# A YOCO trunk on one core: MLPs, second pointwise and output product with the activations stationary, norms by tokens

## The chip, the core and the metric

The kernel runs on one core of one Trainium2 chip. The metric is the device time of one execution in microseconds (us). Every weight comes from HBM in fp32, once.

## What is computed

Two decoder layers on 256 tokens of 2048 features, everything in fp32. Each sub-layer ends with a norm over the features, `x = LN(ALPHA * x + f(x))`:

```python
def conv_module(x, ...):
    a, gate = jnp.split(x @ pw1_w + pw1_b, 2, axis=-1)
    h = a * jax.nn.sigmoid(gate)
    h = causal_depthwise_conv(h, dw_w, width=31) + dw_b
    h = jax.nn.silu(layer_norm(h, ln_g, ln_b))
    return h @ pw2_w + pw2_b

def sq_relu_mlp(x, w1, w2):          # 2048 -> 8192 -> 2048
    return jnp.square(jax.nn.relu(x @ w1)) @ w2
```

Layer 0 is the convolution module, then an MLP. Then K and V are computed once from the residual. Layer 1 is a dilated window attention of 16 heads (queries, three branches, output product `wo`), then an MLP.

## The kernel before

Every product is made in a split form: a weight or activation is the sum of an upper part (`hi`, rounded to the reduced fp32 type) and a lower part (`lo`, the rest), and three products hi*hi, hi*lo and lo*hi are added. Class `Weights` brings a weight in units of 128 x 1024 numbers: SP loads one into `raw`, ACT copies the upper part (`split_piece`, L117), and DVE, or POOL for units that `lo_engine` names, subtracts to get the lower part (L118). `get` keeps six units split ahead of the one in use.

The activations lie with features on partitions: `xres` is [128, 16 tiles, 256 tokens], and a product's input is [128, 16, 512], 256 columns of upper and 256 of lower parts. `fm_group` holds a 128 x 128 block of weights stationary and moves activations past it: for each input tile one matmul of 512 columns by the upper weight (L267) and one of 256 by the lower (L268). A block of 128 output features takes 16 input tiles; the last block of u1 and of the last residual uses three matmuls of 256 columns (`three`, L247 to L249). V alone is made with activations stationary: L690 to L692 move 512 columns of weights, three matmuls for an input tile and a half of the tokens.

An MLP goes through four quarters of its 8192 hidden features: 16 blocks of u1 (`w_1`), squared relu, 16 blocks of u2 (`w_2`) added into `xres` by DVE (L605, L607).

A norm needs sums across partitions. `ln_add` gathers sums on POOL while the last residual is made; then `ln_stats` sums across partitions on TensorE (L341, L343, L344), takes the power -1/2 on POOL (L351), spreads the result by TensorE (L353), and centres the tiles on DVE (L360) and POOL (L362); `ln_apply` scales, splits and writes the next input tile by tile on DVE and ACT (L368, L376, L381). `keep_warm` (L328) issues filler matmuls meanwhile. The last norm of the program is a list written by hand (L784 to L799) that ends with the stores.

The convolution before pw2 keeps DVE and POOL full; its norm ends in the SiLU, where each input tile of pw2 is made by DVE (L583, L584, L589).

## Time and profile before

| | us |
|---|---|
| three runs | 2221.66, 2222.25, 2223.79 (median 2222.25) |
| the profiled execution | 2221.38 |
| its span on the core | 2219.6 |
| TensorE / weight loads busy | 2166.1 / 1911.9 |
| DVE / ACT / POOL busy | 1459.1 / 1048.3 / 426.4 |

The span goes from the first to the last instruction of the core; the profiled execution's own time has 1.8 us around it. A busy TensorE is pipelined, so intervals between starts tell the pace better than the length of one matmul. In a row `xres<-mm,xres` reads "out<-in" by the names in the program; what stands in brackets is the idle time ahead of the instruction and what ended it.

### The profile page before, as it was taken

How to read it: one execution, taken by the hardware profiler on the slowest of the kernel's cores; microseconds unless marked ns; L12 is line 12 of the kernel's file. 1: busy time of each engine (PE TensorE's matmuls, PEld its weight loads, DVE VectorE, ACT ScalarE, POOL GpSimd, SP SyncE). 2: the span in 40 equal slices, each digit the busy share in tenths (PEclk: the TensorE clock that was granted, in tenths of full speed). 3: DMA queues.
4: the chain of work that ended last, by engine and by line, in shares of the span. 5: the costliest groups of instructions: out<-in, count | busy, mean ns of one | idle time of the engine just before them, and what ended most of it. 6: DMA issues, size and time to landing. Idle time of an engine off the chain costs nothing.

```text
span 2219.6 us, 33483 instructions
## 1 busy us (share of the span) xinstructions
PE 2166.1 (98%) x12915; PEld 1911.9 (86%) x12915; DVE 1459.1 (66%) x2206; ACT 1048.3 (47%) x1606; POOL 426.4 (19%) x338
## 2 busy tenths in 40 slices
PE   8899799999999999999999999999999999999997
PEld 7899688888888888888888888888888888888886
DVE  8999967655665665666744466677656656656664
ACT  6557445433443443444554455455434434434443
POOL 5598473000000000006300000640000000000054
PEclk9999999999999999999999999999999999999999
DMA  7364164656855555555465554536555555555552
GB/s 263 109 200 156 64 205 142 197 187 169 258 187 185 188 187 190 190 188 188 132 223 188 189 171 150 182 123 217 189 185 186 190 189 190 188 184 189 185 186 85
DMA packets 113264, 398.07 MB, mean 179 GB/s; under 512 B 12432, under 2 KB 16976, under 8 KB 113104
## 3 DMA queue, kind: packets, MB, share of 16 engines
q1 hardware_dynamic: 111040, 392.79, 54.1%
q10 hardware_dynamic: 2064, 3.15, 1.1%
q8 instruction: 101, 1.65, 0.3%
q14 instruction: 59, 0.48, 0.1%
HBM read 390.64 MB, written 5.24 MB: 178 GB/s over the span
## 4 chain that ended last, share of the span: by engine, by line
PE 86%; DVE 12%; DMA 1%; issue 1%; ACT 0%; SPq 0%; ACTq 0%; DVEq 0%
PE mm L267 51%; PE mm L268 26%; DVE s L467 4%; DVE act L467 2%; DVE o L467 2%; PE mm L692 1%; PE mm L690 1%; PE mm L691 1%; PE mm L249 1%; PE mm L248 1%; PE mm L247 1%; DVE s L471 1%; DVE act L584 0%; DVE xres L381 0%; DMA xres<-in_xt 0%
## 5 line engine op out<-in xcount | busy, mean ns | idle before, releaser
L267 PE MATMUL mm<-act,whi 128*128 128x512 f32 x4928 | 1734.2, 397 | 11.9 <-DVE act L584 6.1
L268 PE MATMUL mm<-act,wlo 128*128 128x256 f32 x4928 | 1380.7, 280 | 0.0
L118 DVE TENSOR_TENSOR wlo<-raw,whi 128x1024 fp32r<-128x1024 f32 (+1 forms) x676 | 835.9, 1239 | 592.4 <-ACT whi L117 570.4
L117 ACT CAST whi<-raw 128x1024 fp32r<-128x1024 f32 (+1 forms) x740 | 769.9, 1047 | 922.7 <-PE mm L267 553.4
L267 PEld LDWEIGHTS mm<-act,whi 128*128 128x128 f32 x4928 | 924.4, 188 | 235.8 <-DVE act L368 6.2
L268 PEld LDWEIGHTS mm<-act,wlo 128*128 128x128 f32 x4928 | 930.3, 189 | 0.8
L612 POOL TENSOR_TENSOR xres<-xres,npiv 128x256 f32<-128x256 f32 x8 | 7.0, 871 | 1585.2 <-ACT npiv L285 1585.2
L247 PE MATMUL mm<-act,whi 128*128 128x256 f32 x704 | 202.5, 288 | 5.9 <-ACT whi L117 5.6
L249 PE MATMUL mm<-act,wlo 128*128 128x256 f32 x704 | 201.2, 286 | 2.3 <-POOL wlo L118 2.1
L248 PE MATMUL mm<-act,whi 128*128 128x256 f32 x704 | 200.6, 285 | 0.1
L118 POOL TENSOR_TENSOR wlo<-raw,whi 128x1024 fp32r<-128x1024 f32 x64 | 155.6, 2464 | 39.9 <-ACT whi L117 39.9
L247 PEld LDWEIGHTS mm<-act,whi 128*128 128x128 f32 x704 | 136.4, 194 | 7.4 <-ACT whi L117 6.1
L249 PEld LDWEIGHTS mm<-act,wlo 128*128 128x128 f32 x704 | 136.2, 193 | 3.4 <-POOL wlo L118 2.5
L248 PEld LDWEIGHTS mm<-act,whi 128*128 128x128 f32 x704 | 136.4, 194 | 0.5 <-DVE act L234 0.3
L605 DVE TENSOR_TENSOR xres<-mm,xres 128x256 f32<-128x256 f32 x128 | 54.0, 423 | 88.1 <-PE mm L268 73.9
L300 POOL TENSOR_TENSOR ln_acc<-ln_acc,xres 128x256 f32<-128x256 f32 x56 | 82.9, 1480 | 95.7 <-DVE xres L607 95.7
L467 DVE SCALAR_TENSOR_TENSOR s<-act,dw,s 128x256 f32<-128x256 f32 x225 | 100.6, 480 | 0.1
L607 DVE TENSOR_TENSOR xres<-mm,xres 128x256 f32<-128x256 f32 x156 | 66.2, 424 | 5.1
L296 ACT ACTIVATE sq<-xres 128x256 f32<-128x256 f32 x60 | 25.2, 420 | 80.1 <-DVE xres L607 26.3
L467 DVE SCALAR_TENSOR_TENSOR act<-act,dw 128x256 f32<-128x256 f32 x56 | 57.5, 1034 | 0.1
L301 POOL TENSOR_TENSOR ln_acc<-ln_acc,sq 128x256 f32<-128x256 f32 x56 | 55.2, 985 | 0.0
L234 DVE TENSOR_TENSOR act<-v,act 128x256 fp32r<-128x256 f32 x120 | 50.2, 419 | 6.6 <-ACT act L233 6.6
(146 smaller groups left out, 1218.2 us busy)
## 6 DMA issues: line engine op xcount, KB each, us to landing
raw<-in_w SPq DMA_DIRECT2D x512, 512.0 KB, 4.2
raw<-in_w_pw SPq DMA_DIRECT2D x94, 512.0 KB, 4.3
raw<-in_w_v SPq DMA_DIRECT2D x32, 512.0 KB, 4.4
raw<-in_w_k SPq DMA_DIRECT2D x32, 512.0 KB, 3.6
raw<-in_w_q SPq DMA_DIRECT2D x32, 512.0 KB, 3.5
raw<-in_w_o SPq DMA_DIRECT2D x32, 512.0 KB, 4.4
scratch<-es ACTq DMA_DIRECT2D x1, 3072.0 KB, 35.2
bt<-scratch SPq DMA_DIRECT2D x16, 128.0 KB, 3.9
```

The source lines that it names most:

```text
L117: self.last_hi = self.nc.scalar.copy(out=hi[:, s], in_=r[:, s])
L118: self.lo_engine[i].tensor_tensor(out=lo[:, s], in0=r[:, s], in1=hi[:, s].bitcast(F32), op=ALU.subtract)
L247: nc.tensor.matmul(out=o, lhsT=hi, rhs=x[:, 0:T], start=kt == 0, stop=False)
L248: nc.tensor.matmul(out=o, lhsT=hi, rhs=x[:, T:2 * T], start=False, stop=False)
L249: nc.tensor.matmul(out=o, lhsT=lo, rhs=x[:, 0:T], start=False, stop=kt == KT - 1)
L267: nc.tensor.matmul(out=acc, lhsT=hi, rhs=x, start=kt == 0, stop=kt == KT - 1)
L268: W.last_mm = nc.tensor.matmul(out=acc[:, T:2 * T], lhsT=lo, rhs=x[:, 0:T], start=False, stop=kt == KT - 1, skip_group_check=True)
L300: nc.gpsimd.tensor_tensor(out=acc[:, 0:T], in0=acc[:, 0:T], in1=z, op=ALU.add)
L301: nc.gpsimd.tensor_tensor(out=acc[:, T:2 * T], in0=acc[:, T:2 * T], in1=sq, op=ALU.add)
L467: nc.vector.scalar_tensor_tensor(out=o, in0=tap, scalar=w, in1=o, op0=ALU.mult, op1=ALU.add)
L605: nc.vector.tensor_tensor(out=y, in0=acc[:, 0:T], in1=y, op=ALU.add)
L607: nc.vector.tensor_tensor(out=y, in0=acc[:, T:2 * T], in1=y, op=ALU.add)
```

## The change

pw2, both MLPs and the output product are now made like V, by `tm_chunk`: an input tile of 128 tokens is stationary and 512 columns of weights move, three matmuls (L299 to L301) for an input tile and a token half s. A chunk is 512 output features and uses eight weight units; four chunks make 2048 features. The residual `xres` is now [128 tokens, 2 halves, 2048 features]. The weights are laid out accordingly on the host, x is loaded a second time by tokens, and the output leaves by tokens.

Since the next product needs features on partitions, `turned` transposes 128 x 512 numbers by four transposes on TensorE (L314), ACT copies the upper part (L317) and DVE subtracts the lower (L318). `after(n, f)` and `tick` put such work n steps (of three matmuls) later. In the MLP the squared relu is ACT's relu and DVE's multiply (L695) on a chunk's half, turned six steps later.

A norm runs along the free axis: `bn_stats` as the chunks come (L617), `bn_aggr`, an addition on DVE (L620, L621) and a power on POOL (L622), then two operations on DVE for each chunk (`apply`, L627 and L629) with gain and bias from rows that SP loads to all partitions. In the last chunk ahead of a norm the last six input tiles are taken first for half 0, then for half 1 (`TAIL`); the first chunk behind it takes eight tiles of half 0 first (`HEAD`). `norm_between` sets after how many steps each apply and each turn comes. The filler matmuls of these norms are gone; those of the convolution's norm stay.

POOL gets the lower part of the first four units of pw2 (`POOL_2`) and of units 3 to 10 of the product behind each of three norms (`POOL_LN`), and the four additions of pw2's bias (L728). The last norm is `final`, by halves, with part of the work on ACT (L839) and POOL (L840, L841). pw1, the convolution, K, Q and the attention's products keep their form.

```diff
+TAIL = 10
+HEAD = 8
...
-TAIL_POOL = 2
+POOL_2 = 4
+POOL_LN = 8
...
+    def tm_units(dram_ap, c, js, lo_engine):
+        return [W.add(dram_ap[c, j, :, h * 1024:(h + 1) * 1024], lo_engine) for j in js for h in range(2)]
+    def mlp_units(layer):
+        return [([tm_units(w_1[layer], 4 * q + c, range(4), nc.vector) for c in range(4)],
+                 [tm_units(w_2[layer], c, range(4 * q, 4 * q + 4), nc.vector) for c in range(4)]) for q in range(NQ)]
+    def on_pool(units):
+        for u in units:
+            W.lo_engine[u] = nc.gpsimd
...
-    u_pw2 = fm_units(w_pw2, groups_of(KT, GRP), nc.vector)
+    u_pw2 = [tm_units(w_pw2, c, range(4), nc.vector) for c in range(4)]
+    on_pool(u_pw2[0][:POOL_2])
...
+    for u in (u_mlp[0][0][0][0], u_v[0], u_mlp[1][0][0][0]):
+        on_pool(range(u[0] + 3, u[0] + 3 + POOL_LN, 1))
...
+    both = [(kt, s) for kt in range(KT) for s in range(2)]
+    one_by_one = lambda a, b: [(kt, s) for s in range(2) for kt in range(a, b)]
+    tail_order = both[:2 * TAIL] + one_by_one(TAIL, KT)
+    head_order = one_by_one(0, HEAD) + both[2 * HEAD:]
+    def tm_chunk(units, x, evacuate, order=both):
+        accs = [bank(ps_mm, "mm") for _ in range(2)]
+        left = [4] * len(units)
+        seen = [0, 0]
+        for kt, s in order:
+            i, k = divmod(kt, 2)
+            hi, lo = W.get(units[i], units[min(j for j, n in enumerate(left) if n)])
+            hi, lo = hi[:, k * 512:(k + 1) * 512], lo[:, k * 512:(k + 1) * 512]
+            xh, xl = x[:, kt, s * P:(s + 1) * P], x[:, kt, T + s * P:T + (s + 1) * P]
+            nc.tensor.matmul(out=accs[s], lhsT=xh, rhs=hi, start=kt == 0, stop=False)
+            nc.tensor.matmul(out=accs[s], lhsT=xh, rhs=lo, start=False, stop=False)
+            nc.tensor.matmul(out=accs[s], lhsT=xl, rhs=hi, start=False, stop=kt == KT - 1)
+            left[i] -= 1
+            if not left[i]:
+                W.drop(units[i])
+            seen[s] += 1
+            if seen[s] == KT:
+                evacuate(s, accs[s])
+            tick()
+    def turned(src, dst, c, s):
+        ps = bank(ps_s, "s")
+        for j in range(4):
+            nc.tensor.transpose(out=ps[:, j * P:(j + 1) * P], in_=src[:, j * P:(j + 1) * P], identity=ident)
+        ps = ps.rearrange("p (j t) -> p j t", j=4)
+        hi, lo = (dst[:, 4 * c:4 * c + 4, o + s * P:o + (s + 1) * P] for o in (0, T))
+        nc.scalar.copy(out=hi, in_=ps)
+        nc.vector.tensor_tensor(out=lo, in0=ps, in1=hi.bitcast(F32), op=ALU.subtract)
...
+        def end(self, s):
+            nc.vector.bn_aggr(out=self.mv[s], in_=self.stats[s])
+            nc.vector.tensor_scalar(out=self.rs[s], in0=self.mv[s][:, 1:2], scalar1=EPS, scalar2=None, op0=ALU.add)
+            nc.gpsimd.tensor_tensor(out=self.rs[s], in0=self.rs[s], in1=npow[:, 0:1], op=ALU.pow)
...
+        def apply(self, s, c):
+            z = xres[:, s, chunk(c)]
+            t = tmp.tile([P, 512], F32, name="t", tag="b")
+            nc.vector.scalar_tensor_tensor(out=t, in0=z, scalar=self.mv[s][:, 0:1], in1=self.g[:, chunk(c)],
+                                           op0=ALU.subtract, op1=ALU.mult)
+            nc.vector.scalar_tensor_tensor(out=z, in0=t, scalar=self.rs[s], in1=self.b[:, chunk(c)],
+                                           op0=ALU.mult, op1=ALU.add)
...
+    def norm_between(norm, dst):
+        def turn_later(n, s, c):
+            after(n, lambda: turned(xres[:, s, chunk(c)], dst, c, s))
+        def at_end(s):
+            norm.end(s)
+            if s == 0:
+                norm.apply(0, 0)
+                after(4, lambda: norm.apply(0, 1))
+                turn_later(5, 0, 0)
+                turn_later(8, 0, 1)
+            else:
+                after(2, lambda: norm.apply(1, 0))
+                after(4, lambda: norm.apply(1, 1))
+                turn_later(5, 1, 0)
+                turn_later(7, 1, 1)
+                for n, c, half in ((8, 2, 0), (10, 2, 1), (12, 3, 0), (15, 3, 1)):
+                    after(n, lambda c=c, half=half: norm.apply(half, c))
+                    turn_later(n + 2, half, c)
+        return at_end
...
-            def evacuate(b, acc, h_hl=h_hl):
...
-            for u in u1:
-                fm_group(u, lambda kt: x_hl[:, kt, :], evacuate, single=u[0][0] == KT - 1)
-            residual(u2, lambda kt, h_hl=h_hl: h_hl[:, kt, :], q == 0, q == NQ - 1, ln)
+                def evacuate(s, acc, c=c, h_hl=h_hl):
+                    r = tmp.tile([P, 512], F32, name="r", tag="a")
+                    v = tmp.tile([P, 512], F32, name="v", tag="b")
+                    nc.scalar.activation(out=r, in_=acc, func=AF.Relu)
+                    nc.vector.tensor_tensor(out=v, in0=acc, in1=r, op=ALU.mult)
+                    after(6, lambda: turned(v, h_hl, c, s))
+                if q == 0 and c == 0:
+                    with tc.manual_schedule(engines={ACT, DVE, POOL}):
+                        tm_chunk(u1[c], x_hl, evacuate, head_order)
+                else:
+                    tm_chunk(u1[c], x_hl, evacuate)
...
+                nc.gpsimd.tensor_tensor(out=y, in0=y, in1=gb[:, 0, c * 1024:(c + 1) * 1024], op=ALU.add)
...
+    def final(norm):
+        def at_end(s):
+            norm.end(s)
+            for c in (0, 1):
+                norm.apply(s, c)
+                nc.sync.dma_start(out=out[s, :, chunk(c)], in_=xres[:, s, chunk(c)])
+            nb = small.tile([P, 1], F32, name="nb")
+            nc.vector.tensor_scalar(out=nb, in0=norm.mv[s][:, 0:1], scalar1=norm.rs[s], scalar2=-1.0,
+                                    op0=ALU.mult, op1=ALU.mult)
+            for c in (2, 3):
+                z = xres[:, s, chunk(c)]
+                if s == 1 and c == 2:
+                    norm.apply(s, c)
+                else:
+                    nc.scalar.activation(out=z, in_=z, func=AF.Identity, scale=norm.rs[s], bias=nb)
+                    nc.gpsimd.tensor_tensor(out=z, in0=z, in1=norm.g[:, chunk(c)], op=ALU.mult)
+                    nc.gpsimd.tensor_tensor(out=z, in0=z, in1=norm.b[:, chunk(c)], op=ALU.add)
+                nc.sync.dma_start(out=out[s, :, chunk(c)], in_=z)
+        return at_end
```

How the change moves instructions, at three places.

TensorE at the norm between pw2 and the first MLP. Before, from the end of pw2 (L247 to L249) to the first MLP matmul (L267); `inv` is the constant of the mean, `s` and `o` are PSUM banks:

```order
L247 MATMUL mm<-act,whi 128x256
L248 MATMUL mm<-act,whi 128x256
L249 MATMUL mm<-act,wlo 128x256
L328 MATMUL s<-whi 128x512 x2
L341 MATMUL mm<-inv,xres 128x1 x2
L343 MATMUL t<-inv,sq 128x1 x2
L344 MATMUL o<-xres,inv 128x256
L328 MATMUL s<-whi 128x512 x3
L353 MATMUL s<-ident,ln_rs 128x128 x2
L328 MATMUL s<-whi 128x512 x6
L267 MATMUL mm<-act,whi 128x512
L268 MATMUL mm<-act,wlo 128x256
```

Now, in the first chunk of the MLP: a step of three matmuls, the turn of a quarter of half 0, and three steps to the next turn:

```order
L314 MATMUL s<-ident,xres 128x128 x4
L299 MATMUL mm<-whi,act 128x512
L300 MATMUL mm<-wlo,act 128x512
L301 MATMUL mm<-whi,act 128x512
L299 MATMUL mm<-whi,act 128x512
L300 MATMUL mm<-wlo,act 128x512
L301 MATMUL mm<-whi,act 128x512
L299 MATMUL mm<-whi,act 128x512
L300 MATMUL mm<-wlo,act 128x512
L301 MATMUL mm<-whi,act 128x512
L314 MATMUL s<-ident,xres 128x128 x4
L299 MATMUL mm<-whi,act 128x512
```

The sums across partitions and the fillers are gone, and groups of four transposes stand among the matmuls of the next product.

POOL from the convolution's norm to the norm behind pw2. Before:

```order
L118 TENSOR_TENSOR wlo<-raw,whi 128x1024
L351 TENSOR_TENSOR ln_rs<-ln_var,npow 128x2
L362 TENSOR_TENSOR act<-act,ln_mc 128x256 x13
L118 TENSOR_TENSOR wlo<-raw,whi 128x1024 x2
L612 TENSOR_TENSOR xres<-xres,npiv 128x256
L619 TENSOR_TENSOR xres<-xres,npiv 128x256
L292 COPY ln_acc<-xres 128x256
```

Now:

```order
L380 TENSOR_TENSOR ln_rs<-ln_var,npow 128x2
L389 TENSOR_TENSOR act<-act,ln_mc 128x256 x13
L728 TENSOR_TENSOR xres<-xres,act 128x1024 x4
L622 TENSOR_TENSOR rs_3132<-rs_3132,npow 128x1
L119 TENSOR_TENSOR wlo<-raw,whi 128x1024 x3
L622 TENSOR_TENSOR rs_3133<-rs_3133,npow 128x1
L119 TENSOR_TENSOR wlo<-raw,whi 128x1024 x5
```

Two weight units of pw2 (L118) became four additions to `xres` (L728), and the eight weight units (L119) of the first MLP stand here, three of them between the powers (L622) of the two token halves.

DVE at the same norm, `t` and `act` being the scratch tile and the next input. Before:

```order
L605 TENSOR_TENSOR xres<-mm,xres 128x256
L349 TENSOR_SCALAR ln_var<-t,ln_m_3988 128x1 x2
L360 TENSOR_TENSOR xres<-xres,o 128x256 x3
L376 TENSOR_TENSOR t<-xres,s 128x256 x2
L381 TENSOR_SCALAR xres<-t,vec 128x256
L376 TENSOR_TENSOR t<-xres,s 128x256
L368 TENSOR_TENSOR act<-xres,act 128x256
L381 TENSOR_SCALAR xres<-t,vec 128x256
L368 TENSOR_TENSOR act<-xres,act 128x256
```

Now, from the statistics of half 1 on:

```order
L620 BN_AGGR mv_3131<-bn_3129 128x2
L621 TENSOR_SCALAR rs_3133<-mv_3131 128x1
L318 TENSOR_TENSOR act<-s,act 128x4x128
L627 SCALAR_TENSOR_TENSOR t<-xres,mv_3131,act 128x512
L629 SCALAR_TENSOR_TENSOR xres<-t,rs_3133,act 128x512
L627 SCALAR_TENSOR_TENSOR t<-xres,mv_3131,act 128x512
L629 SCALAR_TENSOR_TENSOR xres<-t,rs_3133,act 128x512
L318 TENSOR_TENSOR act<-s,act 128x4x128 x2
L627 SCALAR_TENSOR_TENSOR t<-xres,mv_3130,act 128x512
L629 SCALAR_TENSOR_TENSOR xres<-t,rs_3132,act 128x512
L318 TENSOR_TENSOR act<-s,act 128x4x128
L627 SCALAR_TENSOR_TENSOR t<-xres,mv_3131,act 128x512
```

Tile by tile work of 256 columns became pairs of 512 columns, each pair standing behind the lower part (L318) of a turn ahead of it.

## Rows read from the trace of the kernel before

**Rows 1.** The page, part 1: busy time, share of the span and instructions of each engine.

```profile
PE 2166.1 (98%) x12915; PEld 1911.9 (86%) x12915; DVE 1459.1 (66%) x2206; ACT 1048.3 (47%) x1606; POOL 426.4 (19%) x338
```

**Rows 2.** The page, part 4: the chain that ended last, share of the span by engine.

```profile
PE 86%; DVE 12%; DMA 1%; issue 1%; ACT 0%; SPq 0%; ACTq 0%; DVEq 0%
```

**Rows 3.** The page, part 5, weight units: xcount | busy us, mean ns | idle before.

```profile
L118 DVE TENSOR_TENSOR wlo<-raw,whi 128x1024 fp32r<-128x1024 f32 (+1 forms) x676 | 835.9, 1239 | 592.4 <-ACT whi L117 570.4
...
L117 ACT CAST whi<-raw 128x1024 fp32r<-128x1024 f32 (+1 forms) x740 | 769.9, 1047 | 922.7 <-PE mm L267 553.4
...
L118 POOL TENSOR_TENSOR wlo<-raw,whi 128x1024 fp32r<-128x1024 f32 x64 | 155.6, 2464 | 39.9 <-ACT whi L117 39.9
```

**Rows 4.** Timeline of TensorE at the marks: start us, us, engine, line, operation, xcount.

```profile
349.70 0.28 PE L249 MATMUL mm<-act,wlo 128*128 128x256 f32 x1
...
630.07 0.28 PE L249 MATMUL mm<-act,wlo 128*128 128x256 f32 x1
...
811.08 0.29 PE L249 MATMUL mm<-act,wlo 128*128 128x256 f32 x1
...
988.79 0.28 PE L249 MATMUL mm<-act,wlo 128*128 128x256 f32 x1
...
1080.14 0.28 PE L249 MATMUL mm<-act,wlo 128*128 128x256 f32 x1
...
1119.64 0.39 PE L692 MATMUL mm<-whi,act 128*128 128x512 f32 x1
...
1174.26 0.39 PE L267 MATMUL mm<-act,whi 128*128 128x512 f32 x1
...
1387.64 0.47 PE L267 MATMUL mm<-act,whi 128*128 128x512 f32 x1
...
1474.54 0.28 PE L249 MATMUL mm<-act,wlo 128*128 128x256 f32 x1
...
2203.63 0.28 PE L249 MATMUL mm<-act,wlo 128*128 128x256 f32 x1
```

**Rows 5.** Timeline of TensorE, 1304 to 1305 us, inside the attention.

```profile
1304.35 0.49 PE L744 MATMUL t<-ident,p 128*128 128x128 f32 x3
1304.67 0.39 PE L720 MATMUL s<-act,q 128*128 128x128 f32 x2
1304.90 0.60 PE L721 MATMUL s<-act,q 128*128 128x256 f32 x2
```

**Rows 6.** Timeline of DVE and of POOL, 263 to 274 us, the convolution's SiLU.

```profile
263.92 2.29 DVE L583 CAST act<-act 128x256 fp32r<-128x256 f32 x1
266.24 2.44 DVE L584 TENSOR_TENSOR act<-act 128x256 fp32r<-128x256 f32 x1
...
273.59 0.42 DVE L584 TENSOR_TENSOR act<-act 128x256 fp32r<-128x256 f32 x1
...
263.67 4.73 POOL L118 TENSOR_TENSOR wlo<-raw,whi 128x1024 fp32r<-128x1024 f32 x2 [5.25 <-ACT whi L117]
```

**Rows 7.** Groups by line and shape, columns as in rows 3.

```profile
L351 POOL TENSOR_TENSOR ln_rs<-ln_var,npow 128x2 f32<-128x2 f32 x5 | 3.5, 704 | 33.3 <-DVE ln_var L349 33.3
...
L784 DVE TENSOR_TENSOR xres<-xres,o 128x512 f32<-128x512 f32 x2 | 1.3, 683 | 0.6 <-ACT ln_mc L347 0.6
...
L696 ACT COPY act<-mm 128x512 f32<-128x512 f32 x8 | 4.6, 588 | 3.2 <-PE mm L692 2.9
```

**Rows 8.** Timeline of POOL at 155 us: an addition of 512 columns.

```profile
154.86 1.30 POOL L508 TENSOR_TENSOR ln_acc<-ln_acc,act 128x512 f32<-128x512 f32 x1
```

**Rows 9.** Timeline of DVE behind the last product; end of the chain that ended last.

```profile
2204.01 0.43 DVE L605 TENSOR_TENSOR xres<-mm,xres 128x256 f32<-128x256 f32 x1 [6.40 <-PE mm L249]
...
2213.98 0.64 ACTq L909
```

**Rows 10.** Windows: us, PE PEld DVE ACT POOL busy, PEclk, DMA share, GB/s.

```profile
55.00:66.00 11.00, 3.45 (x15) 3.27 (x16) 10.93 (x22) 0.80 (x2) 3.90 (x3) 0.53 0.39 128
...
356.00:362.00 6.00, 4.78 (x24) 3.71 (x25) 6.00 (x12) 3.80 (x7) 6.00 (x8) 1.00 0.00 0
```

More of the change, by code (lines that the diff above doesn't have):

```diff
@@ L273, in fm_group, with after, tick @@
                 W.drop(u)
+    later = []
+    def after(n, f):
+        later.append([n, f])
+    def tick():
+        for e in later:
+            e[0] -= 1
+        while True:
+            e = next((e for e in later if e[0] <= 0), None)
+            if e is None:
+                return
+            later.remove(e)
+            e[1]()
+    both = [(kt, s) for kt in range(KT) for s in range(2)]
[29 more added lines that the diff above has]
+        nc.vector.tensor_tensor(out=lo, in0=ps, in1=hi.bitcast(F32), op=ALU.subtract)
     def ln_begin():
@@ L622, in trunk, with load_rows @@
-    res_tile = lambda kt: xres[:, kt, :]
-    def norm(ln, g, b, unit):
-        rs = ln_stats(ln, res_tile, 3, unit)
-        x_hl = act.tile([P, KT, 512], F32R, name="act")
-        ln_apply(res_tile, rs, g, b, x_hl, unit)
-        return x_hl
+    chunk = lambda c: slice(c * 512, (c + 1) * 512)
+    def load_rows(*which):
+        r = act.tile([P, len(which), D], F32, name="act")
+        with tc.issue_after(W.last_load.ins):
+            for j, w in enumerate(which):
+                nc.sync.dma_start(out=r[:, j, :], in_=rows[w:w + 1, :].to_broadcast([P, D]))
+        return r
@@ new lines, in mlp, with into, at_end_of @@
+            at_end = None
+            if q == NQ - 1:
+                norm = Norm(load_rows(g, g + 1))
+                at_end = at_end_of(norm)
+            if layer == 0 and q == 0:
+                oh = tmp.tile([64, RW], F32, name="oh", tag="a")
+                with tc.issue_after(W.last_load.ins):
+                    nc.sync.dma_start(out=oh, in_=onehot)
+            residual(u2, h_hl, q == 0, norm, at_end)
+            if layer == 0 and q == 0:
+                bias_rows(oh)
+    def into(get_dst):
+        def at_end_of(norm):
+            dst = act.tile([P, KT, 512], F32R, name="act")
+            get_dst.append(dst)
+            return norm_between(norm, dst)
+        return at_end_of
@@ L703, in to_heads @@
         return evacuate
+    assert not later
     for u in u_k:
@@ L820, in _plan @@
+    with tc.manual_schedule(engines={PE}):
+        norm = Norm(load_rows(R_MIXG + 2, R_MIXG + 3))
+        got = []
+        residual(u_o, o_hl, True, norm, into(got)(norm))
+        mlp(1, got[-1], R_MLPG + 2, final)
 def _plan():
```

306 lines of the change are left out of this document (96 added, 210 removed).

## The prediction

> **What bounds the kernel now.** I read the page's busy table first, then the chain of waits, then the groups of instructions, then the timeline stage by stage. TensorE is busy 2166.1 us of the 2219.6 us span [rows 1], and the chain runs through it for 86%, through DVE for 12% [rows 2]; the DVE share is the depthwise convolution, which the change leaves alone. So outside the convolution a stage lasts as long as its matmuls plus what the norm ahead of it makes TensorE wait. The side work is not the bound in the mean: a weight unit of 1024 columns costs ACT 1.05 us and DVE 1.24 us, or POOL 2.46 us [rows 3].
>
> The stages are read from the marks on TensorE [rows 4]. pw2 ends at 349.70, layer 0's MLP at 1080.14, V at 1174.26, the output product runs from 1387.64 to 1474.54, and layer 1's MLP ends at 2203.63. Each of the stretches from one such end to the next begins with a norm.
>
> Two more numbers come from these marks. V is already computed with the activations stationary: from 1119.64 to 1174.26 there are 241 matmuls of 512 columns, 0.2267 us each. And the form with weights stationary has two paces: the last u1 product of quarters 1, 2 and 3 starts at 630.07, 811.08 and 988.79, so one whole quarter takes 181.0 us and the next 177.7.
>
> **The change, part by part.**
>
> *Matmuls.* In the new form one input tile and one token half take 3 matmuls, 0.68 us; a chunk of 512 output features takes 96, or 21.76 us. An MLP has 32 chunks: 3072 x 0.2267 = 696.3 us.
>
> *Transposes.* They are new: 32 groups of four per MLP and 8 per norm. The nearest row is the three transposes in the attention, which hold TensorE from 1304.35 to 1304.67 [rows 5], 0.107 us each; the two L720 products of the same width behind them go to 1304.90, 0.115 each. Four are 0.43 to 0.46 us, and I take 0.46. A norm and its MLP then hold 40 x 0.46 = 18.4 us of them, and 88 groups in the program cost 40 us. Beside this row stands a rule of the Trainium skill, "FP8 and Floating Point Precision", section TensorE Precision Notes: true FP32 takes four passes through the array. By an estimate from that page, 128 columns x 4 at 2.4 GHz would be 0.213 us, 352 transposes 75 us instead of 40, and the sum below would end some 25 us above the time before. The row disagrees by half, and it decides.
>
> *Eviction of u1.* ACT does a relu and later the upper part, DVE a multiply and later the lower part, for 512 columns about 0.6 and 0.7 us each [rows 7], some 2.6 us in all per half chunk of 10.9 us. Beside them stand four weight units, 4.2 us on ACT and 5.0 on DVE. Both fit, and a turn waits six steps (4.1 us) for its operand. I cost it at nothing; without that slack each of 64 turns would stall for the 1.3 us of relu and multiply.
>
> *pw2.* The first chunk follows the SiLU. In the trace DVE ends the SiLU at 273.59 with its 0.42 us [rows 6]. There the DVE cast beside a running POOL product takes 2.29 us, the subtraction behind it 2.44 against 0.42 alone, so each of the two POOL units costs DVE some 2 us. In the order after, DVE gets five more weight units ahead of its last subtraction (5 x 1.24 = 6.2) and POOL runs four adds of 1024 columns instead of two units (some 4 us more of the same lock). So the SiLU ends near 284.2; one tile more and three chunks (1.4 + 65.3) end pw2 at 350.9, before 349.8. Gain **-1.1**; 0 to -5, as the four adds all hit or not.
>
> *Norm and MLP, layer 0.* Before 1080.14 - 349.70 = 730.4 us. After 696.3 + 18.4 + 0.5 (the bias product, priced as two steps) = 715.2 + S, where S is what the norm makes TensorE stand. Gain **15.2 - S**.
>
> *Norm and V.* Before 1174.26 - 1080.14 = 94.1. After 384 x 0.2267 + 8 x 0.46 = 90.7 + S. Gain **3.4 - S**.
>
> *Output product.* Before 86.9 with 16 of its pairs already done inside the attention; after 24 of its 384 are done there, and 360 x 0.2267 = 81.6. Gain **5.3**.
>
> *Norm and MLP, layer 1.* Before 2203.63 - 1474.54 = 729.1; after 714.7 + S. Gain **14.4 - S**.
>
> *Last norm.* Before, the last product is at 2203.63, its eviction starts at 2204.01, and ACT's last work runs at 2213.98 [rows 9], 10.4 us behind. After, the second half's power on POOL (0.70 us [rows 7]) stands behind four POOL operations of 512 columns for the first half, 1.30 us each [rows 8]. Half 0 ends 4.1 us early; eviction, statistics and power take 3 us, an ACT pass 0.6, the four POOL operations 5.3, so the second power ends some 5.5 us after the last product. Behind it DVE has three chunks of 1.3 us and POOL two operations of 1.3, and each shuts the other out as in [rows 6]: 6.6 us plus small gaps, 13.2 in all. Gain **-2.9**; bounds 0 and -5.
>
> **S, the stand of TensorE in each of three norms.** Count from the end of half 0.
> First turn: wait for the eviction (0.4 + 0.7), the statistics (0.6, an estimate by the 0.68 of DVE's L784 on as many columns), two operations on single columns (0.4, an estimate under the 0.70 of POOL's small one), power (0.7) and the last of the two apply operations (0.65, by L784 again) [rows 7], with gaps 3.9 us. TensorE has four steps, 2.7. Stall 1.1 (0 to 2).
> Second half: its power stands on POOL behind three weight units, the order of POOL above shows it. First power done at 3.0, plus 3 x 2.46 = 10.4, power and apply to 11.8. TensorE, with its steps and two turns, is there at 8.8. Stall 3.0 (0 if the units come behind that power).
> Last four exchanges: a turn (0.46), upper part (0.59), lower part (0.64) and the next apply (1.3) go round between TensorE, ACT and DVE in 3.0 us, since DVE takes the apply behind the lower part; the table gives 2 or 3 steps and a turn, 1.8 to 2.5. Stall 0.8 + 1.2 + 1.2 + 0.6 = 3.8 (2 to 11).
> S = **8**. Low end 3: the second power is free and an exchange takes 0.5 less. High end 15.4: three exchanges each meet a POOL unit of 2.46 us.
>
> **Sum.** -1.1 + 15.2 + 3.4 + 5.3 + 14.4 - 2.9 - 3 x 8 = 10.3 us gained. The profiled execution took 2221.4 us; the median of the runs stands 0.9 above it. So 2222.25 - 10.3 = **2212**.
>
> **Rivals.**
> *Slower: POOL shuts DVE out of the norm.* POOL has eight weight units in each norm, five behind the second power, and both apply operations on DVE read two SBUF tensors, the kind that stood 2.3 to 2.4 us in [rows 6]. If a unit starts just ahead of each of the last three applies, S is 15.4 and the sum 34.3 - 46.2 = -11.9: **2234**. It decides from S = 11.4 on, two such hits in each norm. For it: ACT casts the next unit right behind the upper part, so POOL starts about when DVE wants to. Against: DVE's lower part reads PSUM, and a POOL unit that starts there leaves 1.8 us at most. "GPSIMD Engine Reference", §1 Specifications, in the Trainium skill says that POOL shares its SBUF interfaces with VectorE and that instructions with two SBUF inputs contend; the trace agrees, with the 2.44 us above. Chance 0.2.
> *Small stalls.* S = 3, sum 25.3: **2197**. For it: the weight units may be late on POOL since ACT's casts wait for loads or buffers. Against: the exchange is a real ring. Chance 0.2.
> *The clock.* The changed norms drop the filler matmuls. At 55 to 66 us, with TensorE busy 3.45 of 11 us, the granted clock was 0.53; at 356 to 362, busy 4.78 of 6, it was 1.00 [rows 10]. If each norm fell as at 55, three would lose up to 0.47 x 11 = 5.2 us each, 15.5. With half of that, **2220** (2212 to 2228). Against: the stalls are one to three us, with products between. Chance 0.08.
> *A slow pace.* Weights-stationary products fell into a pace 1.9% slower for whole quarters. If the new ones do, 7272 x 0.2267 = 1649 us grow by 30.6 and the sum is -20: **2242**. Against: V's 241 matmuls show one pace. Chance 0.07.
>
> **How the numbers follow.** My forecast has 0.45, with its own range 2204 to 2220. Range of all: 2194 (small stalls, and 3 us for pw2 and the tail) to 2236 (the POOL rival with 2 us over it); the slow pace and the ends of the others are left out. What a measurement can tell from no change is 0.2%, 4.4 us. Faster than 2217.8: 0.37 of the forecast's own 0.45, 0.2 of the small stalls, 0.03 of the clock, 0.60. Slower than 2226.7: 0.15 of the POOL rival, 0.07 of the pace, 0.03 of the rest, 0.25. Between: 0.15.
>
> **What would show it.** Right: the new products at 0.227 us through both MLPs, four transposes at 0.46, quarters of about 177.8 us; TensorE waiting some 8 us in each norm, most of it ahead of the first turn of half 1 and of the last four; the last compute 13 us behind the last product. Wrong: transposes of 0.2 us each, a product pace over 0.23, weight units or u1's evictions that end TensorE's waits inside the MLPs, a granted clock under 1 behind a norm, DVE's apply operations at over 2 us beside POOL.

## The result, and the profile after

| | before | after |
|---|---|---|
| median of four runs | 2223.02 us | 2247.38 us (2240.37 to 2251.42) |
| profiled execution / span | 2221.38 / 2219.6 | 2240.37 / 2238.6 |
| mean granted TensorE clock | 0.994 | 0.982 |

The change makes the kernel slower: ratio 1.0106, 95% interval 1.0076 to 1.0136. The prediction was 2212 us with a range of 2194 to 2236, so both the sign and the range were missed. The profiled execution is the fastest of the four; what the others lost in addition no trace shows.

The page of the kernel after, busy times and the granted clock in 40 slices:

```profile
PE 2153.4 (96%) x10626; PEld 1816.3 (81%) x10626; DVE 1317.6 (59%) x1685; ACT 981.1 (44%) x1317; POOL 262.6 (12%) x142
...
PEclk9999898999999999999899999999999999999998
```

All engines have less to do than in [rows 1], TensorE by 12.7 us, and yet the span is 19.0 us longer. The slices of the granted clock under 9 lie at the start of pw2, at the first two norms and at the end; for more the slices are too coarse, so look at the stages.

Timeline of TensorE, the last product of pw2, of the first MLP, of V, of the output product and of the second MLP:

```profile
352.17 0.63 PE L301 MATMUL mm<-whi,act 128*128 128x512 f32 x1
...
1089.18 0.63 PE L301 MATMUL mm<-whi,act 128*128 128x512 f32 x1
...
1191.03 0.39 PE L301 MATMUL mm<-whi,act 128*128 128x512 f32 x1
...
1491.38 0.39 PE L301 MATMUL mm<-whi,act 128*128 128x512 f32 x1
...
2220.70 0.39 PE L301 MATMUL mm<-whi,act 128*128 128x512 f32 x1
```

Against [rows 4], MLP 0 with its norm took 737.0 us (352.17 to 1089.18) instead of 730.4, V with its norm some 102 instead of 94, MLP 1 with its norm 729.3 instead of 729.1, though the first and the last had been forecast to gain 14 to 15 us less the norm. In the middle of an MLP all is as forecast: in the 695 us from 1525 to 2220, the intervals between starts, less 0.2267 for a product and 0.107 for a transpose, leave 1.2 us. The loss sits in some 40 us around each norm. Timeline of all engines in the first one (rows between left out):

```profile
345.19 1.00 POOL L622 TENSOR_TENSOR rs<-rs,npow 128x1 f32<-128x1 f32 x1 [81.34 <-DVE rs L621]
...
345.50 0.39 PE L301 MATMUL mm<-whi,act 128*128 128x512 f32 x1
346.16 2.33 POOL L119 TENSOR_TENSOR wlo<-raw,whi 128x1024 fp32r<-128x1024 f32 x1
346.22 2.82 DVE L629 SCALAR_TENSOR_TENSOR xres<-t,rs,act 128x512 f32<-128x512 f32 x1 [0.45 <-POOL rs L622]
...
349.14 1.09 PE L314 MATMUL s<-ident,xres 128*128 128x128 f32 x4 [3.26 <-issue]
...
349.88 0.78 PE L299 MATMUL mm<-whi,act 128*128 128x512 f32 x1
...
350.46 0.63 PE L300 MATMUL mm<-wlo,act 128*128 128x512 f32 x1
...
350.88 0.63 PE L301 MATMUL mm<-whi,act 128*128 128x512 f32 x1
...
351.88 4.73 POOL L119 TENSOR_TENSOR wlo<-raw,whi 128x1024 fp32r<-128x1024 f32 x2 [3.38 <-ACT whi L118]
...
354.58 0.15 DVE L621 TENSOR_SCALAR rs<-mv 128x1 f32<-128x1 f32 x1
...
356.56 1.00 POOL L622 TENSOR_TENSOR rs<-rs,npow 128x1 f32<-128x1 f32 x1
...
358.44 0.63 PE L314 MATMUL s<-ident,xres 128*128 128x128 f32 x4 [1.49 <-issue]
...
366.32 2.35 POOL L119 TENSOR_TENSOR wlo<-raw,whi 128x1024 fp32r<-128x1024 f32 x1 [8.76 <-ACT whi L118]
366.50 2.71 DVE L629 SCALAR_TENSOR_TENSOR xres<-t,rs,act 128x512 f32<-128x512 f32 x1
369.36 1.09 PE L314 MATMUL s<-ident,xres 128*128 128x128 f32 x4 [3.50 <-DVE xres L629]
370.10 0.78 PE L299 MATMUL mm<-whi,act 128*128 128x512 f32 x1
```

Read it in this order. At 346.16 POOL takes a weight unit, 0.06 us ahead of DVE's second apply operation, which then lasts 2.82 us instead of 0.75 (at 366.32 POOL is 0.18 us ahead, and the apply lasts 2.71). TensorE waits for that apply, 3.26 and 3.50 us; the row at 349.14 names no engine, but the apply ends at 349.04. And behind each of these two stands (waits of TensorE) the products start 0.43 us apart instead of 0.2267. Of the 24 second apply operations in the three norms, seven take 2.71 to 2.82 us and the rest 0.75. In all seven POOL had started a unit 0.06 to 0.18 us ahead, and the apply ended 0.55 us behind the end of that unit. Where the apply started first (372.49, POOL at 372.89), it took 0.75. I call this the lock. The clock, in windows of the same norm (window and its length in us, PE busy, granted clock, DMA share, GB/s):

```profile
344.00:348.00 4.00, 1.89 (x9) 0.99 0.10 41
348.00:352.00 4.00, 2.85 (x9) 0.50 0.39 131
...
372.00:376.00 4.00, 3.62 (x13) 0.60 0.01 2
```

0.50 is the lower of the two levels, 1.2 GHz, and the pace of 0.43 us fits it. Added up over the intervals of the three norms, TensorE stood 11.2, 11.2 and 14.8 us, and its slow products (what the intervals of products and transposes have over 0.2267 and 0.107 us) cost 5.3, 5.5 and 5.0 us more: 53.0 us where 24 were forecast.

One more stand lies inside MLP 0. ACT, DVE and TensorE at that place:

```profile
565.76 1.05 ACT L118 CAST whi<-raw 128x1024 fp32r<-128x1024 f32 x1 [7.79 <-DMA raw<-in_w]
...
571.71 1.23 DVE L119 TENSOR_TENSOR wlo<-raw,whi 128x1024 fp32r<-128x1024 f32 x1 [1.20 <-ACT whi L118]
572.85 1.28 DVE L695 TENSOR_TENSOR v<-mm,r 128x512 f32<-128x512 f32 x2
...
573.68 1.09 PE L314 MATMUL s<-ident,v 128*128 128x128 f32 x4 [3.19 <-DVE v L695]
```

ACT waited 7.8 us for a load, where 1.7 us between casts is usual. It is beside the 3 MB transfer of the bias rows: in the trace's packets that transfer runs from 547.8 to 581.0, and the weights' queue moves nothing from 547.8 to 560.3. So ACT and DVE were late, u1's relu and multiply stood behind the weight units, and the turn waited for them: with slow products 4.8 us. The trace of the kernel before has the same pause, from 541.2 to 553.5, and TensorE waits for nothing there.

The end of the program, TensorE's last product and POOL and DVE behind it:

```profile
2220.70 0.39 PE L301 MATMUL mm<-whi,act 128*128 128x512 f32 x1
...
2227.59 1.26 POOL L841 TENSOR_TENSOR xres<-xres,act 128x512 f32<-128x512 f32 x1
2228.81 0.55 POOL L622 TENSOR_TENSOR rs<-rs,npow 128x1 f32<-128x1 f32 x1
2229.39 0.75 DVE L629 SCALAR_TENSOR_TENSOR xres<-t,rs,act 128x512 f32<-128x512 f32 x1 [4.22 <-POOL rs L622]
...
2234.36 1.26 POOL L841 TENSOR_TENSOR xres<-xres,act 128x512 f32<-128x512 f32 x1
```

The power of half 1 stands behind the four POOL operations of half 0, as forecast, and DVE waits 4.22 us for it.

### The profile page after: what moved, and what is told of

It reads as the page before. It is cut to its first block, busy times and chain, and to the rows that moved or that the text cites. A ratio compares the mean times of both kernels' runs of the same rounds, so it can differ in the third digit from the quotient of the medians.

```text
span 2238.6 us, 27647 instructions
## 1 busy us (share of the span) xinstructions
PE 2153.4 (96%) x10626; PEld 1816.3 (81%) x10626; DVE 1317.6 (59%) x1685; ACT 981.1 (44%) x1317; POOL 262.6 (12%) x142
## 5 line engine op out<-in xcount | busy, mean ns | idle before, releaser
L119 DVE TENSOR_TENSOR wlo<-raw,whi 128x1024 fp32r<-128x1024 f32 (+1 forms) x656 | 799.6, 1219 | 820.5 <-ACT whi L118 808.4
L118 ACT CAST whi<-raw 128x1024 fp32r<-128x1024 f32 (+1 forms) x740 | 770.2, 1044 | 1006.9 <-PE mm L301 875.0
L299 PE MATMUL mm<-whi,act 128*128 128x512 f32 x2432 | 962.2, 396 | 0.9 <-DVE act L582 0.9
L301 PE MATMUL mm<-whi,act 128*128 128x512 f32 x2432 | 953.9, 392 | 5.8 <-DVE act L583 5.7
L300 PE MATMUL mm<-wlo,act 128*128 128x512 f32 x2432 | 952.7, 392 | 0.0
L301 PEld LDWEIGHTS mm<-whi,act 128*128 128x128 f32 x2432 | 460.2, 189 | 106.5 <-DVE act L583 9.8
L299 PEld LDWEIGHTS mm<-whi,act 128*128 128x128 f32 x2432 | 460.8, 189 | 95.0 <-DVE act L582 2.8
L300 PEld LDWEIGHTS mm<-wlo,act 128*128 128x128 f32 x2432 | 460.7, 189 | 92.9
L622 POOL TENSOR_TENSOR rs<-rs,npow 128x1 f32<-128x1 f32 x8 | 7.5, 938 | 1833.9 <-DVE rs L621 1833.9
L119 POOL TENSOR_TENSOR wlo<-raw,whi 128x1024 fp32r<-128x1024 f32 x84 | 204.3, 2462 | 90.0 <-ACT whi L118 74.3
L259 PE MATMUL mm<-act,whi 128*128 128x512 f32 x512 | 184.3, 404 | 0.0
L245 PE MATMUL mm<-act,whi 128*128 128x256 f32 x512 | 147.7, 288 | 5.7 <-ACT whi L118 5.7
L247 PE MATMUL mm<-act,wlo 128*128 128x256 f32 x512 | 147.2, 288 | 1.9 <-POOL wlo L119 1.9
L246 PE MATMUL mm<-act,whi 128*128 128x256 f32 x512 | 146.7, 287 | 0.0
L260 PE MATMUL mm<-act,wlo 128*128 128x256 f32 x512 | 143.9, 281 | 0.0
L259 PEld LDWEIGHTS mm<-act,whi 128*128 128x128 f32 x512 | 96.3, 188 | 23.5
L245 PEld LDWEIGHTS mm<-act,whi 128*128 128x128 f32 x512 | 100.4, 196 | 6.1 <-ACT whi L118 6.0
L247 PEld LDWEIGHTS mm<-act,wlo 128*128 128x128 f32 x512 | 100.1, 195 | 2.8 <-POOL wlo L119 2.3
L246 PEld LDWEIGHTS mm<-act,whi 128*128 128x128 f32 x512 | 100.3, 196 | 0.1
L260 PEld LDWEIGHTS mm<-act,wlo 128*128 128x128 f32 x512 | 96.7, 189 | 0.4
L317 ACT CAST act<-s 128x512 fp32r<-128x512 f32 x88 | 51.2, 583 | 67.9 <-PE s L314 66.7
```

Source lines behind the costliest of these rows:

```text
L118: self.last_hi = self.nc.scalar.copy(out=hi[:, s], in_=r[:, s])
L119: self.lo_engine[i].tensor_tensor(out=lo[:, s], in0=r[:, s], in1=hi[:, s].bitcast(F32), op=ALU.subtract)
L245: nc.tensor.matmul(out=o, lhsT=hi, rhs=x[:, 0:T], start=kt == 0, stop=False)
L246: nc.tensor.matmul(out=o, lhsT=hi, rhs=x[:, T:2 * T], start=False, stop=False)
L247: nc.tensor.matmul(out=o, lhsT=lo, rhs=x[:, 0:T], start=False, stop=kt == KT - 1)
L259: nc.tensor.matmul(out=acc, lhsT=hi, rhs=x, start=kt == 0, stop=kt == KT - 1)
```

## The experiments

Two theories were open after the trace. **A**: POOL's units hold the apply, and stands of over 3 us bring the clock down. **B**: the exchange between TensorE, ACT and DVE is a ring, or DVE has too much work, and POOL is innocent. Each run's ratio is to the kernel before, run beside it (medians 2221.4 to 2222.6 us).

### No POOL units, fillers, later turns, and the old kernel without its fillers

First, the units off POOL:

```diff
-POOL_LN = 8
+POOL_LN = 0
```

> POOL_LN = 0: the 24 lower parts behind the three norms go from POOL to DVE, nothing else. Theory A (the stands of TensorE in the norms come from POOL: a unit that starts 0.06 to 0.2 us ahead of an apply holds that apply 2.7 to 2.8 us instead of 0.75; these stands of over 3 us then also lower the clock): the apply never takes over 1 us, the stands of 3.4 to 4 us in the norms go to under 2, the half-speed products behind them go, each norm loses 6 to 9 us instead of 16.5 to 19.8, and the time falls by 20 to 30 us, to about 2220. Theory B (the ring of turn, upper part, lower part and apply sets the pace, and DVE's own units of 1.22 us take the place of the lock): each norm still loses 14 to 18 us, and the time moves by under 8 us.

Measured: 2232.13 us, ratio 1.0044 (1.0029 to 1.0059), 15 us under the change. No second apply operation takes over 0.75 us any more. But both theories had a share: the slow products fell to 2.2, 0.6 and 2.2 us in a norm, while TensorE still stood 10.6, 11.2 and 11.1 us. So of the 15 us that the three norms lost less, 10.8 are products at the low clock and 4.3 are stands. The stands hardly fell because others grew: the first turn of half 1 now waited 3.3 us instead of 1.5, since DVE takes weight units (352.40 and 354.14, 1.22 us each) ahead of that half's statistics, and the stand in MLP 0 was 6.5 us instead of 3.2 (the two traces differ by 9.5 us, the medians by 15). In the last four exchanges the timeline shows what TensorE waits for:

```profile
365.32 0.63 PE L314 MATMUL s<-ident,xres 128*128 128x128 f32 x4 [0.36 <-DVE xres L629]
...
365.98 0.59 ACT L317 CAST act<-s 128x512 fp32r<-128x512 f32 x1 [2.98 <-PE s L314]
366.60 0.69 DVE L318 TENSOR_TENSOR act<-s,act 128x512 fp32r<-128x512 f32 x1 [1.43 <-ACT act L317]
...
367.21 0.74 DVE L627 SCALAR_TENSOR_TENSOR t<-xres,mv,act 128x512 f32<-128x512 f32 x1
367.99 0.75 DVE L629 SCALAR_TENSOR_TENSOR xres<-t,rs,act 128x512 f32<-128x512 f32 x1
...
368.89 0.63 PE L314 MATMUL s<-ident,xres 128*128 128x128 f32 x4 [1.55 <-DVE xres L629]
```

Turn, upper part, lower part, two apply operations, turn: 3.57 us round, the next turn is at 372.46, again 3.57 later. The apply does not need the lower part. It only stands behind it in DVE's order.

Second, the change with fillers in the stands (FILL is by chunk and half):

```diff
+    FILL = {(0, 0): 13, (1, 0): 0, (0, 1): 6, (1, 1): 0, (2, 0): 3, (2, 1): 13, (3, 0): 3, (3, 1): 2}
+    def fill(n):
+        spare = bank(ps_o, "o")
+        for k in range(n):
+            for j in range(2):
+                nc.tensor.matmul(out=spare[:, j * P:(j + 1) * P], lhsT=ident, rhs=ident, start=True, stop=True)
```

> Eighty small products of the identity (0.107 us each, 26 + 12 + 6 + 26 + 6 + 4 in each norm) stand ahead of the turns of each of the three norms, sized to fit into the stands of TensorE; POOL keeps its units. Theory A (a stand of over 3 us lowers the granted clock to half and the products behind it cost 5.3 to 5.8 us in each norm): the products behind the stands run at 0.227 us, the granted clock stays at 1.00 through the norms, and the time falls by about 14 to 17 us. Theory B (the clock falls for another reason, or the fillers only push the turns back): the slow products stay, and the time moves by under 4 us or grows by up to 8.5 us in each norm.

Measured: 2264.51 us, 1.0186 (1.0168 to 1.0203), 17 us more than the change where 14 to 17 less were expected. The fillers were twice as long as I had priced them. 26 products of the identity stand as 52 in the trace and take 5.8 us, to the turn at 354.54, 0.223 us each:

```profile
348.74 5.97 PE L658 MATMUL o<-ident 128*128 128x128 f32 x52
```

So the run cannot tell the price of the clock, only where it falls. Windows of the same norm, with the fillers, and at its end behind a stand of 2.09 us (at 382.10) that they had not filled:

```profile
350.00:354.00 4.00, 4.00 (x39) 1.00 0.35 91
...
382.00:386.00 4.00, 3.90 (x12) 0.57 0.40 135
```

Third, later turns in the MLPs:

```diff
-                    after(6, lambda: turned(v, h_hl, c, s))
+                    after(12, lambda: turned(v, h_hl, c, s))
```

> In the MLPs a turn comes 12 steps behind its operand instead of 6 (8.2 us instead of 4.1), nothing else. Theory A (the stand of 3.35 us at 570 us and its slow products come from u1's multiply, which waits on DVE behind weight units that arrive late beside the 3 MB transfer of the bias rows): the stand goes or shrinks under 1 us, 3 to 5 us less. Theory B (the late loads hold the weights themselves): TensorE waits there for a lower part instead, and the time stays within 1.5 us. Either way the three norms keep their loss.

Measured: 2242.67 us, 1.0088 (1.0071 to 1.0105). The stand in MLP 0 is 1.25 us instead of 3.35, and what the MLP lost in all fell by 3.4 us. The time's interval still overlaps with that of the change, so the trace bears this and the time only agrees.

Fourth, the kernel before without the fillers of its three norms:

```diff
-WARM = (2, 3, 6)
+WARM = (0, 0, 0)
```

> The kernel before without the 33 filler products in its three norms between stages, nothing else. Theory A (TensorE's clock falls behind a stand of over 3 us and costs the products behind it): after each of the three norms the first products take 0.7 us per pair instead of 0.35 for some 4 us, 2 to 5 us in each norm, 2229 to 2238 in all. Theory B (the fillers do not matter): within 2 us of 2223.

Measured: 2222.81 us, 1.0002 (0.9993 to 1.0012): no difference. The clock did fall, as theory A says. Window behind the first norm without fillers:

```profile
356.00:360.00 4.00, 3.14 (x10) 0.50 0.00 0
```

and with them, in the kernel before:

```profile
356.00:360.00 4.00, 3.59 (x18) 1.00 0.00 0
```

The pairs go 0.64 us apart from 356.86 on instead of 0.35. But the 42nd pair of the MLP starts 17.28 us behind the first instead of 17.14. In the old form TensorE is ahead of the tiles that DVE hands it and waits for them anyway; a low clock costs where TensorE is the one that is late, and here it is not.

### The ring, or too few steps

The last four applies of a norm one turn ahead, with no POOL units:

```diff
-                for n, c, half in ((8, 2, 0), (10, 2, 1), (12, 3, 0), (15, 3, 1)):
-                    after(n, lambda c=c, half=half: norm.apply(half, c))
-                    turn_later(n + 2, half, c)
+                for a, n, c, half in ((6, 10, 2, 0), (9, 12, 2, 1), (11, 14, 3, 0), (13, 17, 3, 1)):
+                    after(a, lambda c=c, half=half: norm.apply(half, c))
+                    turn_later(n, half, c)
```

> On top of POOL_LN = 0 (2232.1 us): the last four applies of each norm stand one turn earlier in DVE's order, ahead of the lower part of the turn before (steps 6, 9, 11, 13 instead of 8, 10, 12, 15); the turns keep their steps. Theory A (the exchanges are a ring because the apply stands behind the lower part: turn to turn 3.57 us, in the trace at 365.32, 368.89, 372.46): the period falls to 1.8 to 2.6 us, the waits of 1.7, 1.7 and 1.0 us go under 0.7 each, 3 to 4 us less in each norm, about 2222. Theory B (DVE has too much work in the norm, with its units of 1.22 us, whatever the order): the waits come back at other turns, 2228 to 2233.

Measured: 2217.15 us, 0.9965 (0.9952 to 0.9978), 15 us less and now under the kernel before. Nothing is taken off DVE, only its order is changed, and the turns go 1.83 us apart:

```profile
363.08 0.60 PE L314 MATMUL s<-ident,xres 128*128 128x128 f32 x4
...
364.91 0.60 PE L314 MATMUL s<-ident,xres 128*128 128x128 f32 x4
...
366.74 0.60 PE L314 MATMUL s<-ident,xres 128*128 128x128 f32 x4
```

TensorE stood 6.2 us in each norm instead of 11. Theory A of that run holds, and the gain was larger than I expected of it.

Later turns instead, with the order left (turns of half 1 and of the last chunks at 8, 11, 15, 17, 20, 23):

```diff
-                for n, c, half in ((8, 2, 0), (10, 2, 1), (12, 3, 0), (15, 3, 1)):
+                for n, c, half in ((13, 2, 0), (15, 2, 1), (18, 3, 0), (21, 3, 1)):
```

> On top of POOL_LN = 0: the turns of a norm come later among the steps of the next product (9 for the second of half 0; 8, 11, 15, 17, 20, 23 for the others instead of 5, 7, 10, 12, 14, 17), each apply two steps ahead of its turn as before. Theory A (TensorE waits since the order gives each exchange too few steps): a ring of 3.57 us against 2.5, 3.2, 1.8, 2.5, 2.5 leaves some 5.5 us and the first turn of half 1 1.4 instead of 3.5, so 3 to 5 us less in each norm, about 2220. Theory B (the waits are DVE's load and move along): 2228 to 2233.

Measured: 2236.19 us, 1.005 (1.0033 to 1.0067), not separated from the 1.0044 without it. The last four turns still waited 1.8, 1.7, 2.0 and 1.0 us: more steps do not help while each apply waits for the turn before it. And a new wait of 2.9 us comes at the lower part of half 0's second turn. The expectation of 2220 failed.

Both, with the MLPs' turns 12 steps behind (applies at 7, 10, 13, 15, turns at 8, 11, 14, 16, 19, 22):

> POOL_LN = 0, applies one turn ahead, turns later (9; 8, 11, 14, 16, 19, 22), and the MLPs' turns 12 steps behind their operand instead of 6. If order and steps both make the waits: each norm keeps the 1.4 us ahead of its first turn, 1 to 2 us at the first turn of half 1 and little else, 3 to 5 us in all and no half-speed products; the stand near 570 us goes under 2 us; 2200 to 2208, under the kernel before. If DVE's load makes them: 2218 or more.

Measured: 2222.19 us, 0.9999 (0.9989 to 1.0009), worse than the run with the applies ahead alone. This too I had wrong: a later turn is late for its own user, and again by DVE's order. Half 0's second turn comes one step later, so its lower part (L318) now stands behind half 1's first apply, which waits for its power; in the run with the applies ahead it stood in front of that apply and started at 355.71. The third product of a step takes the lower part as its stationary tile and waits. The norms lost 36.1 us in all instead of 24.5, though the stand in MLP 0 fell from 5.3 to 0.8. DVE and TensorE at the first norm:

```profile
357.22 0.75 DVE L629 SCALAR_TENSOR_TENSOR xres<-t,rs,act 128x512 f32<-128x512 f32 x1 [0.44 <-POOL rs L622]
357.89 0.68 DVE L318 TENSOR_TENSOR act<-s,act 128x512 fp32r<-128x512 f32 x1
...
358.63 0.50 PE L301 MATMUL mm<-whi,act 128*128 128x512 f32 x1 [2.91 <-DVE act L318]
```

The same with half 0 ahead by eight tiles, `TAIL = 8` instead of 10:

> The same with TAIL = 8: half 0 runs ahead by eight input tiles (5.4 us) instead of six. If the wait ahead of a norm's first turn is the chain of eviction, statistics, power and apply alone, its 1.4 us go: 3 to 5 us under the run with TAIL = 10. If the four held weight units make the next ones late, TensorE waits for a lower part behind the turn and the time is the same or up to 5 us longer.

Measured: 2214.85 us, 0.9963 (0.995 to 0.9977), 7 us less. The wait ahead of the first turn stayed at 1.35 us, since that turn is still due four steps behind half 0; what shrank is the wait for that lower part of half 0's second turn, in the first norm from 2.9 to 1.8 us, and one of 0.7 us ahead of it went. The weight units were not late: no wait in these norms ends with one. But in the second and third norm a new wait of 1.3 us for a lower part came, so the three norms lost 4.2 us less in all, and the wait that the expectation named did not go.

### POOL alone, and the way to a faster kernel

To part lock and ring: the change with its POOL units, and only the applies ahead.

> The change with its POOL units kept (POOL_LN = 8) and only the last four applies of each norm one turn ahead (as in the run at 2217.2 us, which has no POOL units). Theory A (the lock of POOL is a loss of its own beside the ring): applies of 2.7 to 2.8 us and stands of over 3 us stay, 2228 to 2236, that is 11 us or more above the run without POOL units. Theory B (POOL's units hurt only since the ring waits for every apply): 2215 to 2222.

Measured: 2237.29 us, 1.0068 (1.0053 to 1.0083), against 0.9965 for the same order without the units. With the two other corners, medians in us:

| | apply behind the lower part | apply one turn ahead |
|---|---|---|
| units on POOL | 2247.4 (the change) | 2237.3 |
| units on DVE | 2232.1 | 2217.2 |

By the medians each of the two causes is a loss of its own, POOL's lock 15 to 20 us, the clock behind it included, and the ring 10 to 15. The 10 of the upper row is not separated: the ratios of its two runs, 1.0076 to 1.0136 and 1.0053 to 1.0083, overlap. The lock now meets the applies wherever they stand, POOL and DVE in the first norm:

```profile
366.73 5.19 POOL L119 TENSOR_TENSOR wlo<-raw,whi 128x1024 fp32r<-128x1024 f32 x2 [9.32 <-ACT whi L118]
...
366.91 2.75 DVE L629 SCALAR_TENSOR_TENSOR xres<-t,rs,act 128x512 f32<-128x512 f32 x1
...
370.18 2.28 DVE L627 SCALAR_TENSOR_TENSOR t<-xres,mv,act 128x512 f32<-128x512 f32 x1
```

The lower part (L318), which reads PSUM, starts at 369.58 beside the same POOL units and takes 0.68.

Next, on top of units on DVE and applies ahead: `TAIL = 8`, the first two turns of half 0 at 7 and 10, MLP turns 12 steps behind.

> On top of the run at 2217.2 us (no POOL units, applies ahead): TAIL = 8, the two first turns of half 0 two steps later (7 and 10), MLP turns 12 steps behind. If the wait ahead of the first turn is its chain of operations against four steps: 1.4 us less in each norm and the stand near 565 us (5.3 us) under 2: 2207 to 2212. If held weight units or DVE's load take it back: 2214 to 2220.

Measured: 2208.24 us, 0.9933 (0.9916 to 0.995). The time fell as expected, but not for the reason given. The wait ahead of the first turn is gone, yet the lower part of that turn, now behind an apply and a weight unit on DVE, keeps TensorE waiting for 1.8 us instead, and the three norms together lost 26.2 us in the trace, before 24.5. What shrank is the stand in MLP 0, from 5.3 to 1.4 us.

Then the bias of pw2 off POOL:

```diff
-                nc.gpsimd.tensor_tensor(out=y, in0=y, in1=gb[:, 0, c * 1024:(c + 1) * 1024], op=ALU.add)
...
+                    if bias is not None and c < 3:
+                        nc.vector.tensor_tensor(out=y, in0=y, in1=bias[:, chunk(c)], op=ALU.add)
```

(for the last chunk it is added when the third is evicted).

> The same, and the bias of pw2 is added on DVE behind the evictions of its chunks instead of by four POOL additions beside the SiLU. Theory A (these additions hold DVE's SiLU operations 2.1 to 2.6 us each and TensorE behind them): the waits of 3.6, 0.9, 1.9, 0.9 and 0.9 us and the half-speed products at the start of pw2 go, 5 to 9 us less than the run before this one. Theory B (the weight units on DVE set the end of the SiLU): under 2 us less.

Measured: 2199.43 us, 0.9894 (0.9879 to 0.9909), 9 us less, as theory A has it. The waits of TensorE at the start of pw2 add up to 3.3 us instead of 8.2, its slow products there to 2.1 instead of 6.0. TensorE's last product of pw2, in the run before this one and in this one:

```profile
350.61 0.39 PE L301 MATMUL mm<-whi,act 128*128 128x512 f32 x1
...
342.70 0.39 PE L301 MATMUL mm<-whi,act 128*128 128x512 f32 x1
```

Fillers again, now of transposes, on the run at 2217.2 us:

```diff
+            nc.tensor.transpose(out=spare[:, 0:P], in_=ident, identity=ident)
```

> On top of the run at 2217.2 us: 6 transposes of the identity (0.107 us each) ahead of the first turn of half 0 and 24 ahead of the first of half 1 in each norm, inside the waits of 1.4 and 3.5 us. Theory A (a stand of 3.5 us costs the products behind it a half-speed clock, 0.6 to 3.4 us in each norm in that run): no half-speed products and 3 to 6 us less in all, 2211 to 2214. Theory B (the clock behind short stands costs nothing or falls anyway): within 2 us of 2217.

Measured: 2210.22 us, 0.9946 (0.9931 to 0.9961). The fillers, the turn behind them and a product, in the first norm:

```profile
354.04 2.78 PE L657 MATMUL o<-ident 128*128 128x128 f32 x24
357.51 0.63 PE L314 MATMUL s<-ident,xres 128*128 128x128 f32 x4 [0.69 <-issue]
...
358.20 0.39 PE L300 MATMUL mm<-wlo,act 128*128 128x512 f32 x1
```

24 transposes fill 2.6 us, the turn waits 0.69 us more instead of 3.29 in all, and the products behind it keep 0.23 us. The slow products in the norms fell from 0.6, 3.2 and 2.1 us to 0.6, 0.6 and 0.7, that is by 4.0 of the 4.8 us between the two traces. The intervals of the two ratios overlap a little, so the clock's share is shown by the trace; the 7 us in the medians hold some chance.

Last, the same 24 ahead of the first turn of half 1 in the run with everything else:

> The run at 2199.4 us (no POOL units, applies ahead, TAIL = 8, later MLP turns, bias on DVE) with 24 transposes of the identity (2.6 us) ahead of the first turn of half 1 in each norm, inside the last wait of 2.5 to 3.7 us. Theory A (the half-speed products that are left behind this wait, 0.6 to 3.2 us in each norm, come from the stand alone): no half-speed products in the norms and 3 to 6 us less, 2193 to 2197. Theory B (the fillers hold the turn back as much as they save): 2198 to 2202.

Measured: **2196.89 us**, 0.9889 (0.9873 to 0.9906). The slow products are 2.1, 0.6 and 0.6 us in the three norms (1.7, 0.6 and 3.2 without): in the first the clock still fell, behind a wait of 1.82 us ahead of the fillers. The time is not separated from 0.9894. This run and the one at 2199.4 are the best kernels here, 24 and 22 us under the kernel before and some 50 under the change.

## Why the prediction was wrong, point by point

**Matmuls: right.** 0.2267 us per product through both MLPs, no slow pace as in the old form.

**Transposes: right.** Priced at 0.107 us each, they leave 1.2 us over 128 transposes in the sum over the intervals above; with the intervals around it a turn of four takes 0.45 us, between the 0.43 and the 0.46. The row of the attention decided against the rule of the Trainium skill, "FP8 and Floating Point Precision", section TensorE Precision Notes, and rightly for transposes. For fp32 products the rule holds: the fillers took 0.223 us where the estimate from that page was 0.213.

**pw2: sign wrong, small.** Its last product starts at 352.17; less 3.4 of waiting, 1.5 of slow products and a turn, which belong to the norm, it would be at 346.9, where the kernel before has 349.70 [rows 4]. That is a gain of 2.8 and not a loss of 1.1; in the trace without POOL units, whose pw2 is the same, it is 0.5. DVE's last subtraction of the SiLU starts at 279.50, not near 284.2. What POOL's additions cost was undervalued all the same: I set 4 us on them, and with the bias on DVE the kernel took 9 us less.

**u1's eviction: the step that said "I cost it at nothing" failed**, by 4.8 us in one place. The cover, six steps, was named, but measured by mean loads; one late load used it up.

**S = 8: this is the step that lost the prediction.** It was 16.5, 16.7 and 19.8, of which 11.2, 11.2 and 14.8 are stands and the rest products at the low clock, a term that the sum did not have. The three norms are 29.0 us over the forecast, as much as the whole miss of the trace (19.0 us longer instead of 10.3 shorter); the median of the runs lies 7 us further out, which no trace explains.
Its first turn, 1.1: 3.4 us, as POOL took a unit right behind the first power and locked the first apply.
Its second half, 3.0 for three POOL units ahead of the power: two were there (351.88), the power came 1.8 us late (354.73 to 356.56), and the wait was 1.5, 1.5 and 2.8. The order on POOL was right, but it is not the only limit: without POOL units the power started no earlier (356.99), behind DVE's weight units, and the wait was 3.3.
Its exchanges, 3.8 by a round of 3.0 us: 6.1 us in the first norm; without POOL the round was 3.57. The ring was seen and undersized; that its cause was an order on DVE that could be changed was written in the step ("DVE takes the apply behind the lower part") and not followed up.

**The rivals.** The POOL rival (0.2) and the clock rival (0.08) came true together. I had kept them apart as if one excluded the other. Here they are one chain: the lock makes a long stand, and the clock falls in or behind it; without POOL units the slow products of the norms fell from 15.8 to 5.0 us. The POOL rival's S of 15.4 was not reached by the stands alone. The reason given against the clock, that "the stalls are one to three us", held only under my own S; the long ones of the change were 2.8 to 3.6. The clock cost 15.8 us, just over its upper bound of 15.5. The sum of the parts as measured, each stage between its marks less what norms and stands took in it: 2.8 (pw2) + 14.8 (MLP 0) + 3.7 (V) + 5.2 (output product) + 14.3 (MLP 1) - 53.0 (the norms) - 4.8 (u1's eviction) - 1.9 (last norm) = -18.9, beside the 19.0 by which the span grew. So every stage's own gain came out near its forecast.

**Last norm: about right.** -1.9 for -2.9; the second power ended later than forecast (8.7 us behind the last product, not 5.5), and the last POOL operation started at 13.7 us.

## What to carry to other kernels

Work that is split over engines to fill idle time must be looked at where it starts, not in the mean: a POOL operation on SBUF that starts just ahead of a DVE operation with two SBUF inputs can put nearly its whole length on the critical chain (2.82 us instead of 0.75 here), and DVE was the better place for the same work although POOL stood idle. Where engines hand tiles round, write down each engine's order for two turns and ask of each instruction whether it needs the one ahead of it; here one reordering was worth 15 us with the units on DVE. And rivals that feed each other need a price together.
